# A decoder block on one core: the bias scratch written from all 128 partitions, and the SBUF laid out anew

## The chip, the cores and the metric

The kernel runs on one core of one Trainium2 chip. The metric is device time in microseconds (us), the median of several executions; less is better. "Profile" below is one execution recorded by the hardware profiler, "trace" the list of its instructions, waits and transfers.

## The reference: what is computed

One hybrid decoder block on 256 tokens (SEQ) with a model width of 2048 (D), all in float32:

```python
x = x + 0.5 * swiglu(rms_norm(x, g1), w_gate, w_up, w_down)      # width 2048 -> 5632 -> 2048
h = rms_norm(x, gm)
q, k, v, glu_a, glu_b, gate_a, gate_c = split(h @ w_in)           # 8 heads, two score maps each
o = diff_attention(q1, q2, k1, k2, v, lam, rel_bias_table)        # causal, T5 bias by distance
attn_branch = (rms_norm(o, head_g) * 0.2) @ w_attn_branch
u = causal_depthwise_conv(glu_a * sigmoid(glu_b))                 # 31 taps, 1024 channels
conv_branch = silu(layer_norm(u)) @ w_conv_branch
x = x + (sigmoid(gate_a) * attn_branch + sigmoid(gate_c) * conv_branch) @ w_out
x = x + 0.5 * swiglu(rms_norm(x, g2), ...)                        # a second FFN like the first
return rms_norm(x, final_g)
```

In the attention the score of query position q and key position k gets a bias that depends on the head and on q - k alone: a table of 32 buckets by 8 heads, and -1e30 where k is later than q.

## The kernel before

**Products.** TensorE (PE) does every large product in float32r, a rounded float32. To keep the accuracy, each operand is split into a rounded high part and the rest (hi, lo), and a product is hi*hi + lo*hi + hi*lo. Activations lie transposed as tiles of 128 features by 512 columns: 256 tokens of hi, then 256 of lo, so one such slice is 2 KB in each partition.

- `lin` (L292) multiplies with the weights as the stationary operand. For each k-tile and each of four column tiles it issues a pair: `high` (L305), 512 columns of the activation against `wh`, and `low` (L310), the 256 hi columns against `wl`. It serves both FFNs' up products, the first FFN's down product, the GLU, q, k, and the output projection.
- `lin_tok` (L341) and `tok_products` (L333) turn it round: the activation slice (128 by 128) is stationary and 512 columns of weights move, three matmuls a k-tile (L337 hi*wl, L338 hi*wh, L339 lo*wh). It serves v, the gates, the two branches and the second FFN's down product.

**Weights.** The class `Weights` loads every weight of the model once, in units of 1 MB (four k-tiles by 512 columns), with DMAs on SyncE's queue (SP, L58), three raw buffers `w`. ScalarE (ACT, L87) makes `wh` from a half unit, VectorE (DVE, L88) makes `wl` by subtraction; there are four buffers of each. A new load is issued when a raw buffer has been split. So the splits run a few half units ahead of PE, and the loads two to three units ahead of the splits.

**The order around the bias.** `Side` (L110) runs generators beside the products: each `tick` of `lin` or `lin_tok` advances them at a rate of their own. `bias_rows` (L463) is such a job, one step in ten ticks. It builds in `bias_row` (8 partitions, one for each head, 384 values) the bias by distance, with 32 small copies on GpSimd (POOL, L473), and then issues 8 DMAs on POOL's queue (L477): each takes the 1536 bytes of one head's row, from one partition of SBUF, and writes them 128 times into the DRAM scratch `row_d` (8 x 128 rows of 385 values). Later `bias_load` (L652) reads a head's scratch with rows one value askew, which gives the 128 x 256 tile of biases for a block of queries. POOL also multiplies the gate activations by the norm (L369), in order with these DMAs.

**SBUF.** Pools take their place in the order in which they are made (L142 to L146): `const`, `big`, `wpool`, `work`, `small`. By the allocation of this program, 16 KB of DMA scratch and 128 B of constants come first, then `const` with 2944 B, so `big` begins at byte 19456 of each partition, which is 4 x 4096 + 3072. All tiles of `big` that PE reads are whole multiples of 4 KB long: the residual stream `xT`, the regions P (two tiles of 16 KB: `h1`, `hm`, `mg`, `a2`) and Q (two of 16 KB: `a1`, `qk`, `vo`, `oT`, `cT`, `h2`, `qh`, `ql`), and they all begin at 3072 past a multiple of 4096. `u_sb` (9152 B) lies among them, and so the tiles behind it, `wpool`'s `w`, `wh` and `wl` among them, begin at 4032 past a multiple of 4096: a multiple of 64 B and of nothing larger.

At the very end (L880) the last four half units of weights are not split into `wh` and `wl` but into `qh` and `ql`, which lie in region Q.

`rsqrt` (L248) refines a square root in two scratch tiles of `work`, `rs_v` and `rs_t`; `tmp()` (L236) hands out the five buffers of the tile `t` in turn.

Of the kernel before, what the change touches and what calls it, by code (L numbers as in the profile page):

```python
# [9 lines left out]
F32 = mybir.dt.float32  # L10
# [5 lines left out]
P = 128  # L16
T = 256
D = 2048
FF = 5632
H = 8  # L20
# [5 lines left out]
KU = 4  # L26
KH = 2
NEG = -1e30
LAM_INIT = 0.8 - 0.6 * math.exp(-0.3 * 0)


def bucket(n):
    if n < 16:
        return n
    return min(31, 16 + int(math.log(n / 16) / math.log(8) * 16))
# [98 lines left out]
def block_kernel(  # L134
# [5 lines left out]
    nc = tc.nc  # L140

    const = ctx.enter_context(tc.tile_pool(name="const", bufs=1))  # L142
    big = ctx.enter_context(tc.tile_pool(name="big", bufs=1))
    wpool = ctx.enter_context(tc.tile_pool(name="wpool", bufs=2))
    work = ctx.enter_context(tc.tile_pool(name="work", bufs=2))
    small = ctx.enter_context(tc.tile_pool(name="small", bufs=3))  # L146
    dram = ctx.enter_context(tc.tile_pool(name="dram", bufs=1, space=bass.MemoryType.DRAM))
    psum = ctx.enter_context(tc.tile_pool(name="psum", bufs=5, space=bass.MemoryType.PSUM))
    pmisc = ctx.enter_context(tc.tile_pool(name="pmisc", bufs=3, space=bass.MemoryType.PSUM))
    ctx.enter_context(tc.manual_schedule())  # L150


    groups = [[0, 1, 2, 3], [4, 5, 6, 7], [8, 9, 10]]
# [82 lines left out]
    def tmp():  # L236
        return work.tile([P, T], F32, name="t", tag="t", bufs=5)
# [10 lines left out]
    def rsqrt(dst, src, scale, eps):  # L248

        shape = list(dst.shape)  # L250
        v = work.tile(shape, F32, name="rs_v", tag=f"rsv{shape[-1]}", bufs=1)
        t = work.tile(shape, F32, name="rs_t", tag=f"rst{shape[-1]}", bufs=1)
        nc.vector.tensor_scalar(v, src, scale, eps, ALU.mult, ALU.add)
        nc.scalar.activation(dst, v, AF.Sqrt)
        yield
        nc.vector.reciprocal(dst, dst)
        yield
        nc.vector.tensor_tensor(t, dst, dst, ALU.mult)
        nc.vector.tensor_tensor(t, t, v, ALU.mult)
        yield  # L260
        nc.vector.tensor_scalar(t, t, -0.5, 1.5, ALU.mult, ALU.add)
        nc.vector.tensor_tensor(dst, dst, t, ALU.mult)
        yield
# [11 lines left out]
    def rstd_steps(acc, rstd, n, eps):  # L275
        yield from rsqrt(rstd, mean_d(acc), D / n, eps)
# [181 lines left out]

    row_d = dram.tile([H, P, 385], F32, name="row_d")

    def bias_rows():  # L463
        row = work.tile([H, 384], F32, name="bias_row", tag="s2", bufs=1)

        nc.gpsimd.memset(row[:, 256:384], NEG)
        rel = 0
        while rel < 256:
            end = rel
            while end < 256 and bucket(end) == bucket(rel):  # L470
                end += 1
            b = bucket(rel)
            nc.gpsimd.tensor_copy(row[:, 256 - end:256 - rel], loads["tab"][:, b:b + 1].broadcast_to([H, end - rel]))  # L473
            rel = end
            yield
        for h in range(H):
            nc.gpsimd.dma_start(out=row_d[h:h + 1, :, 0:384], in_=row[h:h + 1].unsqueeze(1).broadcast_to([1, P, 384]))  # L477
            yield


    side.add(bias_rows(), 0.1, delay=256)


# [30 lines left out]

    neglam = small.tile([P, 1], F32, name="neglam", bufs=1)
    U0 = KW - 1
    u_sb = big.tile([P, 8, U0 + T], F32, name="u_sb")
    y_sb = big.tile([P, 8, T], F32, name="y_sb", tag="y")

    def mixer_setup():  # L520
# [6 lines left out]
        nc.vector.tensor_tensor(neglam, e12[:, 0:1], e12[:, 1:2], ALU.subtract)  # L527
        nc.vector.tensor_scalar(neglam, neglam, LAM_INIT, -1.0, ALU.add, ALU.mult)
        nc.vector.tensor_scalar(loads["gh"], loads["gh"], 1.0 - LAM_INIT, None, ALU.mult)
        yield  # L530
# [206 lines left out]
    def attn_finish():  # L737
        nonlocal oT
        rs = small.tile([P, 2 * H], F32, name="rs_o", bufs=1)
        for _ in rsqrt(rs, ss, 1.0 / P, 1e-5):  # L740
            yield
            yield
# [240 lines left out]
```

## Time and profile before

| | us |
|---|---|
| median of 3 runs | 2148.82 (2148.69 to 2148.85) |
| the profiled execution | 2143.47 |
| its span, first to last instruction | 2141.7 |
| PE busy | 2104.0 |
| DVE busy | 1389.4 |
| ACT busy | 1027.7 |
| POOL busy | 189.0 |

The engines run beside each other, so the shares don't add up to the span. "PE" is the matmuls, "PEld" the loads of the stationary operand, which overlap them. Matmuls overlap each other in the trace too: the time that one shows is longer than the distance from its start to the next one's start, and the distance is what a stream of them costs.

### The profile page before, as it was taken

The numbers are of one execution on the slowest core, as the hardware profiler recorded it, in microseconds if no ns is written. First come the engines' busy times: TensorE is split into PE (matmuls) and PEld (weight loads), VectorE is DVE, ScalarE is ACT, GpSimd is POOL, SyncE is SP. The second block draws the span as 40 slices with busy tenths as digits, with TensorE's granted clock in tenths as the row PEclk, the third lists the DMA queues.
The fourth block names the chain that finished last, engine by engine and source line by source line (L and its number), as shares of the span: only waits on it lengthen the run. The fifth ranks groups of instructions, "written<-read, shape, count | busy, mean of one in ns | idle before, by whom it ended". The sixth has DMA issues, their size and how long they took to land. (4 is left out here: it accounts for less than half of the span.)

```text
span 2141.7 us, 28362 instructions
## 1 busy us (share of the span) xinstructions
PE 2104.0 (98%) x11230; PEld 1790.3 (84%) x11230; DVE 1389.4 (65%) x1915; ACT 1027.7 (48%) x1456; POOL 189.0 (9%) x226
## 2 busy tenths in 40 slices
PE   8999999979999999999999999999999999999998
PEld 6888888867888888888778788888888888888887
DVE  8666556635556776789888766665654656545665
ACT  5544344433345555455555744554543444434444
POOL 6101011110011110000000000200100001000011
PEclk9999999989999999999999999999999999999999
DMA  6655555786555555555554555555555555555553
GB/s 236 203 196 180 194 186 189 192 115 214 183 192 179 186 190 197 181 180 178 182 168 169 190 183 177 177 201 192 178 197 180 180 194 193 180 193 177 197 183 132
DMA packets 57446, 395.95 MB, mean 185 GB/s; under 512 B 6864, under 2 KB 6896, under 8 KB 10464
## 3 DMA queue, kind: packets, MB, share of 16 engines
q1 hardware_dynamic: 55872, 390.10, 52.3%
q0 software_dynamic: 1440, 4.03, 2.6%
q8 instruction: 88, 1.44, 0.3%
q14 instruction: 46, 0.38, 0.0%
HBM read 390.43 MB, written 3.67 MB: 184 GB/s over the span
## 5 line engine op out<-in xcount | busy, mean ns | idle before, releaser
L88 DVE TENSOR_TENSOR wl<-w,wh 128x1024 fp32r<-128x1024 f32 x731 | 902.7, 1248 | 607.8 <-ACT wh L87 600.6
L87 ACT ACTIVATE wh<-w 128x1024 fp32r<-128x1024 f32 x731 | 764.8, 1057 | 821.2 <-PE ps_mm L305 546.5
L305 PE MATMUL ps_mm<-h,wh 128*128 128x512 f32 x2816 | 981.7, 396 | 5.9 <-DVE h L229 5.7
L310 PE MATMUL ps_mm<-h,wl 128*128 128x256 f32 x2816 | 762.4, 281 | 3.5 <-DVE wl L88 3.3
L305 PEld LDWEIGHTS ps_mm<-h,wh 128*128 128x128 f32 x2816 | 518.7, 188 | 115.0 <-ACT wh L71 5.7
L310 PEld LDWEIGHTS ps_mm<-h,wl 128*128 128x128 f32 x2816 | 528.1, 188 | 22.3 <-DVE wl L88 5.7
L305 PE MATMUL ps_mm<-a,wh 128*128 128x512 f32 x704 | 246.0, 397 | 18.1 <-ACT wh L87 18.1
L369 POOL TENSOR_TENSOR s_t<-s_t,rstd 128x256 f32<-128x256 f32 x88 | 85.7, 974 | 1201.2 <-ACT s_t L368 1201.2
L310 PE MATMUL ps_mm<-a,wl 128*128 128x256 f32 x704 | 190.9, 282 | 0.5 <-DVE wl L88 0.5
L305 PE MATMUL ps_mm<-hm,wh 128*128 128x512 f32 x512 | 178.9, 396 | 0.0
L305 PEld LDWEIGHTS ps_mm<-a,wh 128*128 128x128 f32 x704 | 130.2, 189 | 45.5 <-ACT wh L87 18.4
L310 PE MATMUL ps_mm<-hm,wl 128*128 128x256 f32 x512 | 138.4, 281 | 0.0
L310 PEld LDWEIGHTS ps_mm<-a,wl 128*128 128x128 f32 x704 | 133.0, 189 | 5.5 <-DVE wl L88 1.0
L337 PE MATMUL ps_mm<-wl,a 128*128 128x512 f32 (+1 forms) x344 | 133.9, 389 | 0.0
L338 PE MATMUL ps_mm<-wh,a 128*128 128x512 f32 (+1 forms) x344 | 133.8, 389 | 0.0
L339 PE MATMUL ps_mm<-wh,a 128*128 128x512 f32 (+1 forms) x344 | 133.8, 389 | 0.0
L337 PE MATMUL ps_mm<-wl,hm 128*128 128x512 f32 x320 | 130.6, 408 | 0.0
L339 PE MATMUL ps_mm<-wh,hm 128*128 128x512 f32 x320 | 126.5, 395 | 0.0
L338 PE MATMUL ps_mm<-wh,hm 128*128 128x512 f32 x320 | 126.4, 395 | 0.0
L305 PEld LDWEIGHTS ps_mm<-hm,wh 128*128 128x128 f32 x512 | 94.4, 188 | 20.4 <-issue 0.7
L571 DVE SCALAR_TENSOR_TENSOR y_sb<-u_sb,cw_sb,y_sb 128x256 f32<-128x256 f32 x240 | 105.3, 478 | 0.0
L354 ACT ACTIVATE rh<-ps_mm 128x256 f32<-128x256 f32 x208 | 77.5, 373 | 45.8 <-PE ps_mm L305 45.7
(192 smaller groups left out, 1808.9 us busy)
## 6 DMA issues: line engine op xcount, KB each, us to landing
w<-in_ffn_w_up_dram SPq DMA_DIRECT2D x88, 1024.0 KB, 4.9
w<-in_ffn_w_down_dram SPq DMA_DIRECT2D x88, 1024.0 KB, 4.8
w<-in_ffn_w_gate_dram SPq DMA_DIRECT2D x85, 1024.0 KB, 4.9
w<-in_w_in_dram SPq DMA_DIRECT2D x72, 1024.0 KB, 4.8
w<-in_w_out_dram SPq DMA_DIRECT2D x16, 1024.0 KB, 4.9
w<-in_w_attn_branch_dram SPq DMA_DIRECT2D x8, 1024.0 KB, 4.8
w<-in_w_conv_branch_dram SPq DMA_DIRECT2D x8, 1024.0 KB, 4.8
w<-in_ffn_w_gate_dram SPq DMA_DIRECT2D x5, 512.0 KB, 8.9
```

Of the source, the lines that this page charges most:

```text
L87: self.nc.scalar.activation(wh, w, AF.Copy)
L88: self.nc.vector.tensor_tensor(wl, w, wh.bitcast(F32), ALU.subtract)
L305: nc.tensor.matmul(ps[ct], lhsT=w, rhs=xs(kt), start=(kt == 0), stop=(kt == nk - 1))
L310: nc.tensor.matmul(ps[ct][:, T:2 * T], lhsT=w, rhs=xs(kt)[:, 0:T], start=False, stop=False)
L337: nc.tensor.matmul(ps, lhsT=hi, rhs=wl[:, kk, :], start=(first and kk == 0), stop=False)
L338: nc.tensor.matmul(ps, lhsT=hi, rhs=wh[:, kk, :], start=False, stop=False)
L339: nc.tensor.matmul(ps, lhsT=lo, rhs=wh[:, kk, :], start=False, stop=(last and kk == KH - 1))
L354: nc.scalar.activation(r, ps[:, T:2 * T], AF.Copy, scale=scale)
L369: nc.gpsimd.tensor_tensor(s, s, rstd, ALU.mult)
L571: nc.vector.scalar_tensor_tensor(y, src, w, y, ALU.mult, ALU.add)
```

## The change

The scratch gets its rows in three steps instead of one. The 8 rows (12 KB) go to a DRAM tile `row_1`; four DMAs read two heads' rows each from there into all 128 partitions of a new SBUF tile `spread` (393 KB each); four DMAs write `spread` to `row_d`, each partition its own copy. `spread` takes the place of region `sga`, which nothing uses until the GLU.

The pools are made in another order: `small` (832 B) moves ahead of `big`, a tile `pad` of 192 B is put behind it, and `u_sb` gets a pool of its own behind `wpool`. With 128 + 2944 + 832 + 192 = 4096, `big` begins at 20480, a multiple of 4096, and so does every tile of `big` and `wpool`. In `rsqrt` the scratch `rs_t` becomes one of the `tmp()` buffers, which makes room.

```diff
--- before.py
+++ after.py
@@ -26,6 +26,7 @@
 KU = 4
 KH = 2
 NEG = -1e30
+PAD = 48
 LAM_INIT = 0.8 - 0.6 * math.exp(-0.3 * 0)
 
 
@@ -140,14 +141,19 @@
     nc = tc.nc
 
     const = ctx.enter_context(tc.tile_pool(name="const", bufs=1))
+    small = ctx.enter_context(tc.tile_pool(name="small", bufs=3))
+
+    pad = ctx.enter_context(tc.tile_pool(name="pad", bufs=1))
     big = ctx.enter_context(tc.tile_pool(name="big", bufs=1))
     wpool = ctx.enter_context(tc.tile_pool(name="wpool", bufs=2))
+    upool = ctx.enter_context(tc.tile_pool(name="upool", bufs=1))
     work = ctx.enter_context(tc.tile_pool(name="work", bufs=2))
-    small = ctx.enter_context(tc.tile_pool(name="small", bufs=3))
     dram = ctx.enter_context(tc.tile_pool(name="dram", bufs=1, space=bass.MemoryType.DRAM))
     psum = ctx.enter_context(tc.tile_pool(name="psum", bufs=5, space=bass.MemoryType.PSUM))
     pmisc = ctx.enter_context(tc.tile_pool(name="pmisc", bufs=3, space=bass.MemoryType.PSUM))
     ctx.enter_context(tc.manual_schedule())
+
+    nc.gpsimd.memset(pad.tile([P, PAD], F32, name="pad"), 0.0)
 
 
     groups = [[0, 1, 2, 3], [4, 5, 6, 7], [8, 9, 10]]
@@ -249,7 +255,7 @@
 
         shape = list(dst.shape)
         v = work.tile(shape, F32, name="rs_v", tag=f"rsv{shape[-1]}", bufs=1)
-        t = work.tile(shape, F32, name="rs_t", tag=f"rst{shape[-1]}", bufs=1)
+        t = tmp()[:, 0:shape[-1]]
         nc.vector.tensor_scalar(v, src, scale, eps, ALU.mult, ALU.add)
         nc.scalar.activation(dst, v, AF.Sqrt)
         yield
@@ -458,6 +464,7 @@
 
 
 
+    row_1 = dram.tile([H, 384], F32, name="row_1")
     row_d = dram.tile([H, P, 385], F32, name="row_d")
 
     def bias_rows():
@@ -473,8 +480,15 @@
             nc.gpsimd.tensor_copy(row[:, 256 - end:256 - rel], loads["tab"][:, b:b + 1].broadcast_to([H, end - rel]))
             rel = end
             yield
-        for h in range(H):
-            nc.gpsimd.dma_start(out=row_d[h:h + 1, :, 0:384], in_=row[h:h + 1].unsqueeze(1).broadcast_to([1, P, 384]))
+        nc.gpsimd.dma_start(out=row_1, in_=row)
+        yield
+        spread = big.tile([P, H, 384], F32, name="spread", tag="sga")
+        for h in range(0, H, 2):
+            nc.gpsimd.dma_start(out=spread[:, h:h + 2], in_=bass.AP(tensor=row_1.tensor, offset=row_1.offset + h * 384,
+                                                                  ap=[[0, P], [1, 2 * 384]]))
+            yield
+        for h in range(0, H, 2):
+            nc.gpsimd.dma_start(out=row_d[h:h + 2, :, 0:384].rearrange("h p c -> p h c"), in_=spread[:, h:h + 2])
             yield
 
 
@@ -514,7 +528,7 @@
 
     neglam = small.tile([P, 1], F32, name="neglam", bufs=1)
     U0 = KW - 1
-    u_sb = big.tile([P, 8, U0 + T], F32, name="u_sb")
+    u_sb = upool.tile([P, 8, U0 + T], F32, name="u_sb")
     y_sb = big.tile([P, 8, T], F32, name="y_sb", tag="y")
 
     def mixer_setup():
```

## Rows read from the trace of the kernel before

**Rows 1.** The page, first lines: span; PE's busy time, share and instructions.

```profile
span 2141.7 us, 28362 instructions
PE 2104.0 (98%) x11230; PEld 1790.3 (84%) x11230; DVE 1389.4 (65%) x1915; ACT 1027.7 (48%) x1456; POOL 189.0 (9%) x226
```

**Rows 2.** Waits of PE over the whole span: us in total, times, longest.

```profile
PE ps_mm L305 <- ACT wh L87: 18.1, 1, 18.1
```

**Rows 3.** Waits of all engines, 440 to 500 us.

```profile
ACT wh L87 <- DMA w<-in_ffn_w_down_dram: 21.2, 2, 20.9
```

**Rows 4.** Timeline of PE, 466 to 492 us: start, duration, instruction, idle before it.

```profile
467.35 0.28 PE L310 MATMUL ps_mm<-a,wl 128*128 128x256 f32 x1
485.71 0.79 PE L305 MATMUL ps_mm<-a,wh 128*128 128x512 f32 x1 [18.08 <-ACT wh L87]
...
490.55 0.46 PE L305 MATMUL ps_mm<-a,wh 128*128 128x512 f32 x1
```

**Rows 5.** DMA, 448 to 483 us: queue's share of 16 engines; issues, median us to landing.

```profile
q0 software_dynamic: 331, 0.98, 78.0%
...
w<-in_ffn_w_down_dram SPq DMA_DIRECT2D x2, 1024.0 KB, 32.4
```

**Rows 6.** DMA issues of the whole span: count, KB each, median us to landing.

```profile
w<-in_ffn_w_up_dram SPq DMA_DIRECT2D x88, 1024.0 KB, 4.9
...
out_dram<-x SPq DMA_DIRECT2D x8, 256.0 KB, 2.7
...
row_d<-bias_row POOLq DMA_DIRECT2D x8, 192.0 KB, 17.2
...
fg<-in_final_norm_g_dram POOLq DMA_DIRECT2D x1, 1024.0 KB, 6.8
```

**Rows 7.** Timeline of POOL, 400 to 480 us.

```profile
403.30 1.09 POOL L477 DMA_DIRECT2D row_d<-bias_row  x2 [0.30 <-POOL bias_row L473]
437.59 0.74 POOL L369 TENSOR_TENSOR s_t<-s_t,rstd 128x256 f32<-128x256 f32 x1 [33.20 <-ACT s_t L368]
...
444.95 2.60 POOL L477 DMA_DIRECT2D row_d<-bias_row  x5
```

**Rows 8.** Timeline of PE, 2108.5 to 2119 us, weights moving: first and last of two runs.

```profile
2108.30 0.39 PE L339 MATMUL ps_mm<-wh,a 128*128 128x512 f32 x1
...
2111.10 0.39 PE L339 MATMUL ps_mm<-wh,a 128*128 128x512 f32 x1
...
2113.17 0.39 PE L339 MATMUL ps_mm<-qh,a 128*128 128x512 f32 x1
...
2116.57 0.39 PE L339 MATMUL ps_mm<-qh,a 128*128 128x512 f32 x1
```

**Rows 9.** Timeline of PE, 2119 to 2123 us: first and last of nineteen 256-column matmuls.

```profile
2120.17 0.28 PE L339 MATMUL ps_mm<-wh,a 128*128 128x256 f32 x1
...
2122.21 0.28 PE L339 MATMUL ps_mm<-wh,a 128*128 128x256 f32 x1
```

**Rows 10.** Two stretches of `lin` alone: length, then busy us and count by engine.

```profile
50.00:185.00 135.00, 135.00 (x773) 118.04 (x772) 84.75 (x110) 66.92 (x100) 24.17 (x42) 1.00 0.56 191
575.00:710.00 135.00, 135.00 (x767) 117.53 (x766) 80.61 (x104) 62.87 (x92) 11.61 (x12) 1.00 0.54 187
```

**Rows 11.** Lines 305 and 337 on PE: count, min/median/max ns, first and last start.

```profile
L305 PE MATMUL ps_mm<-h,wh x2816: 387/396/767, 5.7 to 2066.3; 128*128 128x512 f32 x188
...
L337 PE MATMUL ps_mm<-wl,hm x320: 392/394/587, 911.4 to 1202.5; 128*128 128x512 f32 x160
```

**Rows 12.** Two stretches with the convolution on DVE, columns as in rows 10.

```profile
870.00:1050.00 180.00, 180.00 (x925) 148.05 (x923) 157.36 (x288) 90.28 (x152) 2.14 (x4) 1.00 0.53 182
1050.00:1200.00 150.00, 149.44 (x675) 118.53 (x674) 127.99 (x231) 87.44 (x138) 1.07 (x2) 1.00 0.50 174
```

**Rows 13.** Timeline of POOL, 0 to 6 us.

```profile
1.26 0.20 POOL L214 MEMSET ones<- 128x128 f32 x1
4.12 0.61 POOL L244 TENSOR_TENSOR acc<-xT 128x256 f32<-128x256 f32 x1 [2.67 <-DMA xT<-in_x_dram]
```

## The prediction, made before the change was run

> **What bounds the kernel now.** I read the page's first lines, then the waits of PE, then the one stretch in which PE waits, then how fast PE goes where it doesn't. PE is busy 2104.0 of 2141.7 us, and DVE, the next, 1389.4 [rows 1]. So the end is set by PE, and a change can pay in two ways alone: PE waits less, or its matmuls follow each other faster. Of waits there is one of size: 18.1 us, once, for ACT's `wh` [rows 2]. What idle time is left to PE is small.
>
> The wait lies at 467 us. Between the matmul at 467.35 and the next at 485.71 PE does nothing, and ACT, which PE waits for, itself waits 20.9 us for a weight load [rows 3, 4]. That load took 32.4 us to land, where its kind takes 4.9 [rows 5, 6]. What filled the DMA engines is POOL's queue, 78% of all sixteen from 448 to 483 us, with 0.98 MB [rows 5]: 0.98 MB in 35 us is 28 GB/s. These are the bias DMAs. Two were issued at 403, then POOL stood 33 us behind a gate multiplication that waits for ACT, and five went out within 2.6 us from 445 on [rows 7]. Each reads one partition. 192 KB at 28 GB/s is 7 us, so the five hold the DMA engines until about 483, and PE starts again at 485.7.
>
> The Trainium skill says the same of a single partition: on its page "SBUF — State Buffer", section "Door 1: The DMA port swizzle", four partitions on one port move 27.6 GB/s and all 128 move 328. The 28 GB/s of this trace agrees.
>
> **How fast PE goes.** This is where the second half of the change must act, so I looked for a place in the trace of before where only the address differs. There is one, at the end of the kernel. `tok_products` runs there on the same stationary tile `a2`, with 512 columns moving, first from `wh`/`wl`, then from `qh`/`ql`, with nothing else changed in the loop. From `wh`/`wl` twelve steps take 2.80 us, 233.3 ns each. From `qh`/`ql` fifteen steps take 3.40 us, 226.7 ns each [rows 8]. The first lie at 4032 past a multiple of 4096, which is only a multiple of 64; the second at 3072, a multiple of 1024. So a moving read from the badly placed tiles costs 6.7 ns a matmul. With 256 columns a step from `wl`/`wh` is 113.3 ns (eighteen in 2.04 us), half of 226.7 [rows 9]: there the placement costs nothing, presumably because the stationary load, from the well placed `a2`, takes as long.
>
> Now `lin`. Its moving tiles are well placed (regions P and Q), its stationary ones are `wh`/`wl`. 773 matmuls overlap 135 us, and 767 in another stretch [rows 10]. Taking off the two that reach over the edges, a pair takes 350 ns in the one and 353 in the other. Well placed it should be a step of 512 and one of 256, 226.7 + 113.3 = 340.0 ns. The excess is 10 to 13 ns, and two reads at 6.7 ns are 13.3. So both forms fit one price: about 6.7 ns for each read from the `w` tiles, a little of it hidden in the first stretch.
>
> **The change part by part.**
>
> 1. *The stall.* 485.71 - 467.35 - 0.12 = 18.2 us. After it the matmuls run at half speed for a while: from 485.71 to 490.55 there are six pairs, 4.84 us where 2.1 would do [rows 4], so 2.7 us more. Sum 21 us, if the new transfers don't starve the loads. They are 12 KB, then four reads of 393 KB, then four writes of 393 KB, which is twice the bytes. But a broadcast row into 128 partitions (`fg`, 1 MB) lands in 6.8 us beside the loads, and 256 KB out of 128 partitions lands in 2.7 [rows 6]. By these the 3.15 MB take some 1.6 x 6.8 + 6 x 2.7 = 27 us of latency one after the other, but far less of the engines' time, and they are spread from 403 to about 460 as POOL comes free. The loads were starved only after 22 us of nearly full engines (445 to 467), so I take no stall; the bound on the other side is half of it kept, 10 us. New waits: POOL waits for `row_1` before the reads, and for the reads before the writes, a few us each. Behind them stands nothing before 600 us but the gate multiplications of 437 to 445 us, and their result is read a whole `lin` later (64 pairs, 22 us). Nobody reads `row_d` before 781 us.
>
> 2. *`lin`.* 2816 + 704 + 512 + 256 = 4288 pairs (line 305 has four groups, of which one is shown) [rows 11]. 11.5 ns each, the middle of the two stretches, is 49 us; by the two ends 43 to 56. If only the moving read matters, it is nothing.
>
> 3. *`lin_tok`.* 328 + 320 + 64 + 64 = 776 k-steps with 512 columns from `wh`/`wl` (line 337 has five groups, of which one is shown) [rows 11], three matmuls each: 2328 x 6.67 = 15.5 us.
>
> 4. *The rest.* The memset of `pad`: 0.2 us on POOL, as a larger one takes [rows 13], before a wait of 2.67 us for `x`; nothing. `rs_t` from the `tmp` ring: a DVE step may wait for the user four buffers back, which is done long before; 0 to 1 us. No instruction of PE is added or taken away. DVE is the cover that gets thin: where the convolution runs it is busy 157 of 180 and 128 of 150 us, 87 and 85% [rows 12]. With PE 3% faster this is 90%. If that made PE wait, it would take back at most the gain of these 330 us, 10 us; I take none.
>
> Sum: 21 + 49 + 15.5 = 86 us (rounded). Against the profiled execution's own 2143.5 this gives 2057.5; the median of the runs lies 5.3 us above that execution, and I keep the difference: 2148.8 - 86 = 2063.
>
> **The rivals.**
>
> *A. Stall gone, every read at the good price.* 2063; with the bounds above 2054 to 2075.
>
> *B. The good price is only partly reached in `lin`,* because 512 and 256 columns alternate there. For it: the nine steps between the two runs of rows 8, just behind the change of tiles, take 2.07 us, 230 ns each, so a rhythm has to settle. Against: in `lin` the tile and the rhythm are the same for hundreds of pairs, and the excess in the second stretch is just two reads' price. Half of `lin`'s gain: 2148.8 - 21 - 15.5 - 24.5 = 2088.
>
> *C. The address doesn't matter;* the 6.7 ns belong to the part of the memory in which `wpool` lies, or to what else goes on in it (loads and splits write there). The 256-column row speaks for it a little, since there the bad address costs nothing. Against: line 337 has a median of 394 ns in the gates' stage, with loads and splits beside it, and shows the same 0.39 us at the end of the kernel [rows 8, 11], and the two runs of rows 8 are neighbours. Only the stall goes: 2148.8 - 21 = 2128. The Trainium skill would have it so: "TensorE: Matmul & The Clock Gate", section "Back-to-back issue gap", gives a distance that depends on the columns alone, and "SBUF — State Buffer", section "SBUF: two separate sides", gives PE ports of its own that wait for nobody. By the first rule 512 columns would be an estimated 215.8 ns; the trace has 226.7 and 233.3 and so doesn't agree.
>
> *D. Slower: the reads get in each other's way.* With all tiles at multiples of 4096 the stationary and the moving read of one matmul begin in the same place of their 4 KB. If this made the two streams meet, it would be in the main loop of every stage. No row shows such a meeting, so its price is bounded by nothing here; I take one bad read's 6.7 ns more for each pair and each matmul of `lin_tok`: (4288 + 2328) x 6.67 = 44 us, less the stall's 21: 2148.8 + 23 = 2172. It decides from 21 us / 6616 = 3.2 ns on. Against: in the second run of rows 8 the distance between the stationary and the moving address takes several multiples of 1024, among them multiples of 4096, at one speed.
>
> *E. The scratch doesn't do what it says:* if not the read of one partition but the writing of 1024 short rows to DRAM were the 28 GB/s, the same rows are written now and the stall stays. Against: the final output leaves at 256 KB in 2.7 us [rows 6], though in longer rows. With the good price of the reads 2063 + 21 = 2084.
>
> **How the numbers follow.** A 0.54, B 0.15, C 0.17, D 0.06, E 0.08. The likeliest is A: 2063. A, B and E end below 2100 and hold 0.77, so the range has to take in C: 2054 to 2128. Its lower end is A with `lin` at 56 us and two us of rounding. 0.2% is 4.3 us, about what a measurement of this kernel tells from no change. A, B, C and nearly all of E are faster by more, 0.93; slower is D with a rest, 0.05; within it 0.02.
>
> **What would show it.** The stall: no row of PE waiting for `wh` near 467 us, and weight loads landing in 5 to 10 us there. If E is right, the writes of `spread` take as long as the 17.2 us of the old ones. The reads: the medians of L305 (396 ns) and L337 (394) [rows 11] fall by about 7 ns, steps of L337 are 226.7 ns in all stages, and a pair of L305 and L310 takes 340 ns, so 50 to 185 us holds about 795 matmuls instead of 773. If C is right the medians don't move; if B is right L337 moves and L305 only half. What would make the prediction wrong most is that the stationary read has no such price, since for it there is no pair of rows that differs in the address alone.

## The result, and the profile after

The changed kernel takes 2118.66 us (2117.05 to 2119.28), against 2148.84 (2148.69 to 2149.89) for the kernel before on the same chip: a ratio of 0.9857 [0.984, 0.9874], 30 us less where 86 were forecast. The time lies in the stated range, 2054 to 2128, but the gain is about a third of the forecast one. The profiled execution took 2118.52 us.

In the code after, L311 is `high` (before L305), L316 `low` (L310), L343 to L345 are the three matmuls of `lin_tok` (L337 to L339), and L88 and L89 are the splits.

The page's first lines, answering [rows 1]. The span is 25 us shorter and PE still fills it, DVE's busy time is what it was:

```profile
span 2116.7 us, 28368 instructions
PE 2097.1 (99%) x11230; PEld 1790.2 (85%) x11230; DVE 1389.5 (66%) x1915; ACT 1027.7 (49%) x1456; POOL 190.0 (9%) x228
```

All of PE's waits (us in total, times, longest), answering [rows 2]:

```profile
PE ps_mm L311 <- DVE h L235: 6.0, 2, 5.8
PE ps_mm L316 <- DVE wl L89: 3.0, 4, 1.9
PE ps_mg L837 <- DVE sg L832: 0.9, 1, 0.9
PE ps_mean L273 <- DVE acc_c L594: 0.9, 1, 0.9
```

The 18.1 us for `wh` are gone. The DMA view of 448 to 483 us, answering [rows 5]: POOL's queue takes 19.5% of the engines for 2.37 MB where it took 78.0% for 0.98, and weight loads land in 4.9 us instead of 32.4. The writes of `spread` carry 384 KB in 9.2 us; the old writes needed 17.2 for 192 KB [rows 6].

```profile
q0 software_dynamic: 614, 2.37, 19.5%
...
w<-in_ffn_w_down_dram SPq DMA_DIRECT2D x7, 1024.0 KB, 4.9
row_d<-spread POOLq DMA_DIRECT2D x4, 384.0 KB, 9.2
spread<-row POOLq DMA_DIRECT2D x2, 384.0 KB, 6.8
```

Now PE's pace. Three stretches of the kernel after: the two of [rows 10], `lin` alone, and one of `lin_tok` alone. Columns: length, then busy us and count of PE, PEld, DVE, ACT and POOL, granted clock, DMA share, GB/s.

```profile
50.00:185.00 135.00, 135.00 (x766) 117.14 (x766) 85.40 (x111) 66.17 (x99) 25.62 (x43) 1.00 0.57 194
575.00:710.00 135.00, 135.00 (x766) 117.10 (x765) 84.46 (x114) 65.81 (x99) 12.32 (x13) 1.00 0.54 185
...
1845.00:1880.00 35.00, 35.00 (x157) 28.96 (x156) 17.13 (x15) 13.43 (x14) 0.00 (x0) 1.00 0.59 202
```

And the third stretch in the kernel before:

```profile
1845.00:1880.00 35.00, 35.00 (x152) 28.05 (x151) 18.89 (x19) 14.22 (x15) 0.00 (x0) 1.00 0.56 190
```

`lin_tok` went from 152 matmuls in 35 us to 157: less the two at the edges, 233.3 ns each before and 225.8 after. (Such a count is good to one matmul: 1.5 ns for `lin_tok` here, 0.5 ns for a pair of `lin` in 135 us.) `lin` did not get 795 matmuls into 135 us, but 766, a pair in 353.4 ns. That is the slower of the two paces that it had before (773 and 767), now in both stretches.

The durations tell the same, answering [rows 11] (min/median/max ns). `lin_tok`'s median falls from 394 to 389 ns, `lin`'s rises from 396 to 398:

```profile
L311 PE MATMUL ps_mm<-h,wh x2816: 388/398/765, 5.8 to 2042.2; 128*128 128x512 f32 x188
```
```profile
L343 PE MATMUL ps_mm<-wl,hm x320: 387/389/577, 897.6 to 1184.9; 128*128 128x512 f32 x160
```

Two stretches of PE's timeline (start, duration) show where `lin`'s gain was lost. The first is a piece of `lin`, the second the end of the kernel, which answers [rows 8, 9]:

```profile
639.77 0.40 PE L311 MATMUL ps_mm<-h,wh 128*128 128x512 f32 x1
640.01 0.28 PE L316 MATMUL ps_mm<-h,wl 128*128 128x256 f32 x1
640.12 0.40 PE L311 MATMUL ps_mm<-h,wh 128*128 128x512 f32 x1
640.37 0.28 PE L316 MATMUL ps_mm<-h,wl 128*128 128x256 f32 x1
640.49 0.40 PE L311 MATMUL ps_mm<-h,wh 128*128 128x512 f32 x1
640.72 0.28 PE L316 MATMUL ps_mm<-h,wl 128*128 128x256 f32 x1
...
641.89 0.40 PE L311 MATMUL ps_mm<-h,wh 128*128 128x512 f32 x1
```
```profile
2094.81 0.28 PE L343 MATMUL ps_mm<-wl,a 128*128 128x256 f32 x1
...
2096.85 0.28 PE L345 MATMUL ps_mm<-wh,a 128*128 128x256 f32 x1
...
2102.44 0.39 PE L343 MATMUL ps_mm<-wl,a 128*128 128x512 f32 x1
...
2104.93 0.39 PE L345 MATMUL ps_mm<-wh,a 128*128 128x512 f32 x1
```

At the end of the kernel (where `qh`/`ql` hold the first four of the last eight half units, so that `wh`/`wl` come back behind them) 512 columns from `wl`/`wh` are at the good pace: eleven steps in 2.49 us, 226.4 ns. But seventeen steps of 256 columns take 2.04 us, 120.0 ns each, where before it was 113.3 [rows 9]. The placement that makes 512 columns 6.7 ns faster makes 256 columns 6.7 ns slower, and a pair of `lin` is one of each: by these steps 233.3 + 113.3 = 346.7 ns before and 226.7 + 120.0 = 346.7 after. (They are steps with the weights moving; in `lin` the weights are stationary. Experiment 2 has the steps of `lin` itself for the kernel after; for the kernel before no run has them.) In `lin` neither sum is reached: six pairs from 639.77 to 641.89 us take 2.12 us, 353.3 ns, and the steps of the high go 0.24, 0.25, 0.23 us, again and again.

### The profile page after: what moved, and what is told of

It is laid out like the page before. It is cut to its first block, busy times and chain, and to the rows that moved or that the text cites. A ratio compares the mean times of both kernels' runs of the same rounds, so it can differ in the third digit from the quotient of the medians.

```text
span 2116.7 us, 28368 instructions
## 1 busy us (share of the span) xinstructions
PE 2097.1 (99%) x11230; PEld 1790.2 (85%) x11230; DVE 1389.5 (66%) x1915; ACT 1027.7 (49%) x1456; POOL 190.0 (9%) x228
## 5 line engine op out<-in xcount | busy, mean ns | idle before, releaser
L89 DVE TENSOR_TENSOR wl<-w,wh 128x1024 fp32r<-128x1024 f32 x731 | 902.7, 1248 | 581.4 <-ACT wh L88 578.6
L88 ACT ACTIVATE wh<-w 128x1024 fp32r<-128x1024 f32 x731 | 765.3, 1057 | 794.7 <-PE ps_mm L311 553.2
L311 PE MATMUL ps_mm<-h,wh 128*128 128x512 f32 x2816 | 986.7, 400 | 6.0 <-DVE h L235 6.0
L316 PE MATMUL ps_mm<-h,wl 128*128 128x256 f32 x2816 | 762.8, 282 | 3.3 <-DVE wl L89 3.0
L311 PEld LDWEIGHTS ps_mm<-h,wh 128*128 128x128 f32 x2816 | 519.5, 189 | 119.4 <-ACT wh L72 5.7
L316 PEld LDWEIGHTS ps_mm<-h,wl 128*128 128x128 f32 x2816 | 532.7, 189 | 22.8 <-DVE wl L89 5.2
L311 PE MATMUL ps_mm<-a,wh 128*128 128x512 f32 x704 | 245.4, 398 | 0.0
L316 PE MATMUL ps_mm<-a,wl 128*128 128x256 f32 x704 | 189.9, 281 | 0.0
L311 PE MATMUL ps_mm<-hm,wh 128*128 128x512 f32 x512 | 180.1, 400 | 0.0
L311 PEld LDWEIGHTS ps_mm<-a,wh 128*128 128x128 f32 x704 | 129.2, 188 | 28.2
L316 PE MATMUL ps_mm<-hm,wl 128*128 128x256 f32 x512 | 138.4, 281 | 0.0
L316 PEld LDWEIGHTS ps_mm<-a,wl 128*128 128x128 f32 x704 | 132.9, 189 | 4.7
L343 PE MATMUL ps_mm<-wl,a 128*128 128x512 f32 (+1 forms) x344 | 132.1, 384 | 0.0
L345 PE MATMUL ps_mm<-wh,a 128*128 128x512 f32 (+1 forms) x344 | 132.1, 384 | 0.0
L343 PE MATMUL ps_mm<-wl,hm 128*128 128x512 f32 x320 | 129.5, 405 | 0.0
L345 PE MATMUL ps_mm<-wh,hm 128*128 128x512 f32 x320 | 125.3, 392 | 0.0
L311 PEld LDWEIGHTS ps_mm<-hm,wh 128*128 128x128 f32 x512 | 94.4, 188 | 21.4 <-issue 0.7
```

The source lines that it names most:

```text
L88: self.nc.scalar.activation(wh, w, AF.Copy)
L89: self.nc.vector.tensor_tensor(wl, w, wh.bitcast(F32), ALU.subtract)
L311: nc.tensor.matmul(ps[ct], lhsT=w, rhs=xs(kt), start=(kt == 0), stop=(kt == nk - 1))
L316: nc.tensor.matmul(ps[ct][:, T:2 * T], lhsT=w, rhs=xs(kt)[:, 0:T], start=False, stop=False)
L343: nc.tensor.matmul(ps, lhsT=hi, rhs=wl[:, kk, :], start=(first and kk == 0), stop=False)
L345: nc.tensor.matmul(ps, lhsT=lo, rhs=wh[:, kk, :], start=False, stop=(last and kk == KH - 1))
```

## The experiments

Each time stands beside the kernel before on the same chip: medians of 2146.41, 2145.84, 2149.18 and 2147.8 us in four groups (runs from 2142.62 to 2150.2). The changed kernel stands beside 2148.84 in a group of its own, so a difference of two or three us against it says little. "Pair" is a high and a low of `lin`, read from 50 to 185 us as above; `lin_tok` from 1845 to 1880 us. Where it says "the starts give", it is the mean of the distances from start to start within `lin` or `lin_tok`, without those that hold a wait or another matmul (over 280 ns for 512 columns, over 140 for 256).

**1. One part at a time.** Against the changed kernel, first the new scratch in the old layout, then the new layout with the old scratch:

```diff
-    small = ctx.enter_context(tc.tile_pool(name="small", bufs=3))
-    pad = ctx.enter_context(tc.tile_pool(name="pad", bufs=1))
...
-    upool = ctx.enter_context(tc.tile_pool(name="upool", bufs=1))
+    small = ctx.enter_context(tc.tile_pool(name="small", bufs=3))
...
-        t = tmp()[:, 0:shape[-1]]
+        t = work.tile(shape, F32, name="rs_t", tag=f"rst{shape[-1]}", bufs=1)
...
-    u_sb = upool.tile([P, 8, U0 + T], F32, name="u_sb")
+    u_sb = big.tile([P, 8, U0 + T], F32, name="u_sb")
```

```diff
-        nc.gpsimd.dma_start(out=row_1, in_=row)
...
-        for h in range(0, H, 2):
-            nc.gpsimd.dma_start(out=row_d[h:h + 2, :, 0:384].rearrange("h p c -> p h c"), in_=spread[:, h:h + 2])
+        for h in range(H):
+            nc.gpsimd.dma_start(out=row_d[h:h + 1, :, 0:384], in_=row[h:h + 1].unsqueeze(1).broadcast_to([1, P, 384]))
```

> The scratch in three steps, on the layout of before. Theory of two separate parts: only the stall at 467 us goes, so 21 us by the trace of before and up to 26 if the runs without the profiler stalled longer: 2122 to 2128 us, no row of PE waiting for wh near 467 us, steps of lin_tok still 233.3 ns, pairs of lin between 349 and 354 ns. If the new transfers starve the loads in part, a shorter wait stays and the time is 2130 to 2140.

> The new layout with the old scratch, each row written from one partition. Theory: the stall of 18 us comes back and lin_tok keeps its steps of 226.7 ns, with pairs of lin at 353.3 as in the changed kernel: 2118.7 + 21 to 26 = 2140 to 2145 us. If the layout took away part of the stall by itself, 2119 to 2130.

The scratch alone: 2125.05 us (2121.67 to 2127.53), ratio 0.99 [0.9878, 0.9922], 21 us less. The layout alone: 2139.46 (2137.68 to 2140.49), 0.9967 [0.9956, 0.9978], 7 us less, and the stall is back. From PE's waits:

```profile
PE ps_mm L311 <- ACT wh L88: 18.4, 1, 18.4
```

The two parts add up to the whole (21 + 7 of 30) as far as the intervals tell, so neither takes much from the other, and the missing gain is the layout's. With the new layout in both, the scratch is worth 2139.46 - 2118.66 = 20.8 us.

**2. The order of `lin`, not its addresses.** If the pace is a rhythm of 512 and 256 columns, another order must move it at the same addresses. First, runs of two (per column tile high, high, low, low):

```diff
-                for i in range(len(pair) * KH):
-                    if pair[0] * KH + i < nk - 1:
-                        high(ct, i)
-                        low(ct, i)
-                    else:
-                        low(ct, i)
-                        high(ct, i)
+                for i in range(0, len(pair) * KH, KH):
+                    two = range(i, i + KH)
+                    for f in (high, low) if pair[0] * KH + i + KH < nk else (low, high):
+                        for j in two:
+                            f(ct, j)
```

> The changed kernel, with the order of matmuls in lin changed: for each column tile two of 512 columns, then two of 256, instead of one and one. Theory R (the cost is in the change between the widths, whatever the address): half as many changes, so a pair falls from 353.3 to about 347 ns, 4288 x 6 = 26 us, 2093 us. Theory S (each stationary read from wh and wl costs its 6.7 ns whatever the order): 353 ns and 2119 us.

2102.41 us (2101.46 to 2102.74), 0.9799 [0.9784, 0.9814]: 16 us faster than the changed kernel. The stretch of 50 to 185 us holds 776 matmuls, a pair in 348.8 ns:

```profile
50.00:185.00 135.00, 135.00 (x776) 117.87 (x775) 86.14 (x112) 67.25 (x100) 25.61 (x43) 1.00 0.58 197
```

Then runs of eight, all highs of a half unit over the four column tiles and then all lows:

```diff
+            for i in range(0, len(pair) * KH, KH):
+                end = pair[0] * KH + i + KH == nk
+                for f in (low, high) if end else (high, low):
+                    for ct in range(4):
+                        for j in range(i, i + KH):
+                            f(ct, j)
```

> The changed kernel, with eight matmuls of 512 columns over the four column tiles and then eight of 256. Theory R: within a lin a pair comes to 340 (226.7 + 113.3) to 346.7 ns (226.7 + 120.0, the steps at the end of the changed kernel), 28 to 57 us, 2062 to 2091; the four results of a lin are now ready within 2 us, so at its end PE may wait for banks of PSUM, which could take back up to 1 us for each of 68 lins. Theory S: 353 ns inside a lin, 2119 us or more.

2196.11 us (2195.38 to 2196.61), 1.0236 [1.022, 1.0252]: slower, and for another reason. Its largest waits of PE:

```profile
PE ps_mm L311 <- DVE t L361: 29.4, 42, 1.3
PE ps_mm L311 <- DVE s_t L361: 25.9, 41, 0.9
```

At the end of a `lin` all four result tiles in PSUM, the memory that PE writes to, now become ready together, and the next `lin` waits until they are read out (L361). Between these waits the starts of the matmuls give 349.1 ns a pair, no better than runs of two. So longer runs bring the pair no further, and the order at the end of a `lin` matters by itself.

This run also has what the trace of before lacked, long streams of one width in `lin`, with the weights stationary. In the new layout the sixth to eighth high of a run start 227 ns apart and the lows behind the first 119 to 121 ns (some 400 of each): the 226.7 and 120.0 of the kernel's end hold for `lin` too. The first five highs behind a run of lows take 228 to 236 ns; that is where the change of widths is paid.

**3. Which tiles' placement.** The `wl` tiles alone moved 64 B on, in the order of the changed kernel and in runs of two:

```diff
+    padl = ctx.enter_context(tc.tile_pool(name="padl", bufs=1))
+    lpool = ctx.enter_context(tc.tile_pool(name="lpool", bufs=2))
+    nc.gpsimd.memset(padl.tile([P, 16], F32, name="padl"), 0.0)
-        wl = self.pool.tile([P, KH, CK], F32R, name="wl", tag="wl", bufs=self.bufs)
+        wl = self.lpool.tile([P, KH, CK], F32R, name="wl", tag="wl", bufs=self.bufs)
```

> The changed kernel with the four wl tiles moved by 64 B (wh and all else stay). Theory M (the stationary and the moving read of neighbouring matmuls meet, and what counts is the difference of their addresses: streams of 512 columns want 0, as the 226.7 against 233.3 ns of lin_tok, streams of 256 want 64, as the 113.3 of the old layout's end against the 120.0 of the new one's): in lin the steps of 256 columns, whose stationary tile is wl, get cheaper, a pair falls from 353.3 to 340 to 347 ns, 28 to 57 us, and lin_tok's third matmul with wl moving goes back to 233.3, 776 x 6.7 = 5 us: 2067 to 2096. Theory R alone (only the alternation of widths costs, the address of the stationary tile nothing): lin stays at 353 and the time is 2124.

> As the one before, and two matmuls of 512 columns, then two of 256, as in the run with runs of two (2102 us, 349.0 ns a pair). Theory M: 340 to 345 ns, 2102 - 17 to 39 + 5 = 2068 to 2090. Theory R alone: 349, 2107.

2125.51 us (2124.01 to 2126.76), 0.9902 [0.9885, 0.992], and 2115.91 (2115.49 to 2117.49), 0.9859 [0.9845, 0.9874]: 7 and 13.5 us slower than with `wl` in its place. Theory M is refuted, since nothing got faster. R alone comes near in the first run (2124), but not in the second (2107). A stretch of `lin` and one of `lin_tok` of the first:

```profile
50.00:185.00 135.00, 135.00 (x767) 116.94 (x766) 85.37 (x111) 66.42 (x99) 25.59 (x43) 1.00 0.58 195
...
1845.00:1880.00 35.00, 35.00 (x153) 28.32 (x152) 18.11 (x17) 12.84 (x13) 0.00 (x0) 1.00 0.57 198
```

The pair stays at 352.9 ns (in runs of two the starts give 350.0), and `lin_tok` goes back to 35/151 = 231.8 ns. There the starts give 231 to 232 ns for each of its three lines, though `wl` is read by one of them alone: 2328 x 4.5 = 10 us, where the expectations had 5. So here the pace belongs to the stream of the three lines and not to the one matmul whose operand was moved.

**4. All of PE's tiles 64 B on.** Does the multiple of 4 KB count, or only how the tiles lie to each other?

```diff
-PAD = 48
+PAD = 64
```

> The changed kernel with all of big and wpool moved by 64 B together, so that every tile begins 64 past a multiple of 4096 and the differences stay. Theory M (differences): steps of 226.7 in lin_tok and pairs of 353.3, 2118 us. Rival (the moving read itself wants a multiple of 128 or more): steps of 233.3 in lin_tok as in the kernel before, 2118 + 13 to 15 = 2133.

One run, 2119.33 us, within the changed kernel's runs but for 0.05 us. Both paces are the changed kernel's:

```profile
50.00:185.00 135.00, 135.00 (x766) 117.09 (x765) 85.53 (x111) 65.93 (x98) 25.61 (x43) 1.00 0.57 193
...
1845.00:1880.00 35.00, 35.00 (x156) 28.96 (x156) 17.14 (x15) 13.79 (x13) 0.00 (x0) 1.00 0.57 195
```

None of PE's large tiles begins at a multiple of 4 KB here, nor of 128 B. So the multiple does nothing; what is left is the difference between the addresses.

**5. Runs of two in the old layout** (the first kernel of 1 with the order of 2):

> The old layout with the new scratch (2125 us, pairs between 349 and 354 ns) and lin in runs of two. If the gain of runs of two does not need the new layout, a pair falls to about 349 ns on the mean, some 4 ns x 4288 = 16 us, 2108 us, and the runs scatter less. If it needs it, 2120 to 2127.

2098.95 us (2097.47 to 2099.24), 0.9778 [0.9763, 0.9792]: 20 us faster than the changed kernel, with its layout left out.

```profile
50.00:185.00 135.00, 135.00 (x784) 118.78 (x783) 86.96 (x112) 67.55 (x102) 25.65 (x43) 1.00 0.58 197
...
1845.00:1880.00 35.00, 35.00 (x152) 28.20 (x151) 16.98 (x16) 13.78 (x13) 0.00 (x0) 1.00 0.55 194
```

A pair in 135/391 = 345.3 ns, faster than the new layout in any order tried, and faster than either case of the expectation; `lin_tok` at 233.3. For `lin` the old placement is the better one.

**6. The difference, several in one kernel.** Gaps between the activation regions, with `lin` in runs of two, so that one execution has several differences against the same weights. First four of them:

```diff
+    gaps = {"P1": 384, "Q0": 64, "Q1": 32, "end": 32}
+    def gap(tag):
+        n = gaps.pop(tag, 0)
+        if n:
+            nc.gpsimd.memset(big.tile([P, n // 4], F32, name=f"gap_{tag}"), 0.0)
     def region(r, i, shape, dtype, name):
+        gap(f"{r}{i}")
```

> The changed kernel with `lin` in runs of two (as in the run in which both highs go ahead of both lows), and with small gaps between the four activation regions, so that region P's first tile (h, a2 of k-tiles 0 to 7) begins 512 B below wh and wl (modulo 4 KB), P's second tile 128 B below, Q's first tile (a1, oT) 64 B below and Q's second (a1, cT) 32 B below. All four cases stand in one run, against the same wh and wl. If the pace hangs on the difference modulo 128 B, as the runs so far allow: 512 and 128 go like difference 0 (349.0 ns a pair in lin, 226.7 ns a matmul in lin_tok), 64 like the old layout (345.2 and 233.3), and 32 like one of them or between. If a larger unit counts (the old layout differed by 960, and only multiples of 4096 have been tried as 'difference 0' in lin), 512 and 128 go otherwise too. If not the difference but the place of the weights or of the activation counts, all four go at one pace. By the middle one the time is about 2102 to 2104 us: only a1 (704 pairs) and 384 of the lin_tok matmuls change pace.

One run, 2108.76 us, where 2102 to 2104 was expected (the expectation counts `a1` alone on Q; `h2` lies there too, with 1408 pairs more). In `lin_tok` on `a2` at the kernel's end, the first tile (512 B below) has 156 matmuls in 35 us, 227.3 ns; the second (128 B below) takes ten steps in 2.32 us, 232 ns (L349 to L351 are the three matmuls of `lin_tok` here):

```profile
2035.00:2070.00 35.00, 35.00 (x156) 29.01 (x155) 23.65 (x25) 19.04 (x20) 0.00 (x0) 1.00 0.57 192
```
```profile
2092.78 0.39 PE L350 MATMUL ps_mm<-wh,a 128*128 128x512 f32 x1
...
2095.10 0.39 PE L351 MATMUL ps_mm<-wh,a 128*128 128x512 f32 x1
```

So 512 goes as 0 does, and 128 does not: modulo 128 falls. By the starts of all of `lin_tok` it is 227.7 ns at 512 B below, 232.5 at 128, 228.9 at 64 and 233.3 at 32. For `lin` the starts give 348.3 ns a pair at 512 B below, 350.4 at 128, 347.3 at 64 and 350.8 at 32; at difference 0, in the runs of two of experiment 2, they give 348.5 on the first tile of a region and 349.5 on the second. The old layout's difference is -960, which modulo 512 is 64 ahead, not 64 below; if that is the whole of it, -448, which is 64 ahead modulo 512 too, must bring both of its paces back:

```diff
+    gaps = {"Q0": 64, "end": 448}
```

> The changed kernel with `lin` in runs of two and 64 B between regions P and Q; 448 B behind Q bring wh and wl back to P's phase. Region Q (a1, oT, cT, h2) then begins 64 B ahead of wh and wl modulo 512 (the old layout's difference, -960, is the same modulo 512 and 1024), region P (h1, hm, mg, a2) 0 ahead. If the difference modulo some 512 B sets the pace, both paces stand in one run: lin on P (2176 pairs) at 349.0 ns a pair, lin on Q (2112 pairs) at the 345.2 of the old layout in runs of two; lin_tok on P 226.7 ns, on Q (oT and cT, 384 matmuls) 233.3. Against the 2102.4 us of runs of two in the new layout this is 2112 x 3.8 ns = 8.0 us less and 384 x 6.67 ns = 2.6 us more: 2097, about the 2099 of the old layout in runs of two. If the sign or the whole distance counts and not the difference modulo 512, Q goes at another pace, as the 347.2 ns at 64 B below.

2097.0 us (2095.82 to 2097.62), 0.9765 [0.975, 0.9779], the 2097 expected. Stretches of `lin` on P, `lin` on Q, `lin_tok` on P and (1175 to 1210 us) `lin_tok` on Q:

```profile
50.00:185.00 135.00, 135.00 (x776) 117.80 (x775) 84.98 (x111) 67.53 (x100) 24.14 (x42) 1.00 0.57 191
...
1662.00:1797.00 135.00, 135.00 (x785) 118.73 (x784) 84.79 (x111) 66.28 (x98) 11.64 (x12) 1.00 0.55 188
1845.00:1880.00 35.00, 35.00 (x157) 28.96 (x156) 16.77 (x16) 13.79 (x13) 0.00 (x0) 1.00 0.56 184
```
```profile
1175.00:1210.00 35.00, 35.00 (x152) 28.20 (x151) 22.68 (x22) 22.08 (x24) 0.00 (x0) 1.00 0.59 194
```

On P 348.8 and 225.8 ns, on Q 344.8 and 233.3: the paces of the new and of the old layout side by side in one execution, from one gap of 64 B. (On Q the changed kernel has 227 ns by the starts, so it is not the stage that makes `lin_tok` slow there.) It is the fastest kernel of the study, though its interval and that of experiment 5 overlap.

**7. `wl` alone by 448 B,** so that the low's activation is 64 ahead of it modulo 512 and the high's at difference 0:

```diff
-    nc.gpsimd.memset(padl.tile([P, 16], F32, name="padl"), 0.0)
+    nc.gpsimd.memset(padl.tile([P, 112], F32, name="padl"), 0.0)
```

> The changed kernel with `lin` in runs of two and the wl tiles alone 448 B further on (the earlier run had them 64 B further on: 349.8 ns a pair, 232.0 ns in lin_tok). The low product's activation is then 64 B ahead of wl modulo 512, as in the old layout, the high product's at difference 0. If each matmul had a pace of its own by its own two addresses, the lows would be those of the old layout and the highs those of the new one, and a pair would be 226.7 to 233 + 113.3 to 116, below 349. If the pace belongs to the sequence as a whole, as the run with wl by 64 showed for lin_tok (all three lines slowed, though the addresses of two were unchanged), the pair stays near 349 and lin_tok near 232, and the time near the 2115.9 of that run.

2100.65 us (2099.27 to 2101.32), 0.9783 [0.9767, 0.98]. 779 matmuls in 135 us, a pair in 347.5 ns, and `lin_tok` 35/153 = 228.8 ns:

```profile
50.00:185.00 135.00, 135.00 (x779) 118.31 (x778) 85.17 (x111) 67.88 (x100) 24.30 (x43) 1.00 0.58 193
...
1845.00:1880.00 35.00, 35.00 (x155) 28.71 (x153) 17.64 (x17) 13.77 (x13) 0.00 (x0) 1.00 0.57 197
```

Neither expectation fits whole. Paces between the two layouts' are possible, and the pair does not get near the 340 ns that the best step of each width would give.

## Why the prediction was wrong

*Step 1, the stall: right.* 21 us forecast, 21 measured (the scratch alone, 2146.41 to 2125.05; in the new layout 20.8). The loads land in time during the new transfers. E is refuted by POOL's queue, 2.37 MB in 19.5% of the engines' time where 0.98 MB took 78.0%: the same rows, written from 128 partitions, don't hold the engines.

*Step 3, `lin_tok`: right in size, not in its reason.* 233.3 to 226.7 was forecast for 2328 matmuls, 15.5 us. The starts of all matmuls of the three lines give a mean of 233.3 before and 227.5 after, 2328 x 5.8 = 13.5 us; the rest would be the slower steps behind a change of tiles or widths. But the prediction laid the 6.7 ns on tiles that begin at a multiple of 64 B only. In experiment 4 they do, and the pace is the good one. What set the two runs of [rows 8] apart is the difference: `qh`/`ql` and `a2` both lie at 3072, at a difference of 0, `wh`/`wl` at one of -960. The change brought the difference to 0 together with the multiple of 4 KB, so the sum came out.

*Step 4: right.* DVE, which was to get thin, makes PE wait for 0.9 us at one place of the convolution (`acc_c`), 0.6 before.

*Step 2, `lin`: wrong, in size and in sign.* 49 us less was forecast. By the starts of its matmuls a pair takes 352.9 ns after, against a mean of 351.3 before: 4288 x 1.6 = 7 us more. The step that failed is "both forms fit one price: about 6.7 ns for each read from the `w` tiles". It was worked out by taking 340.0 ns as the well placed pair, and a part of that sum, the 113.3 ns of 256 columns, came from a row of the badly placed tiles [rows 9]. The prediction read the row as "there the placement costs nothing". There was no row of 256 columns at the new placement; when there was one, it said 120.0. Of the 13.3 ns between 340.0 and the 353.3 of the timeline above, this is 6.7. The other 6.7 is what the alternation costs, a term that the likeliest case put at nothing: runs of two take 4.6 of it away at the same addresses (353.4 to 348.8 ns, experiment 2).

So the missing gain has two halves: the fast 512 and the fast 256 do not meet in the new layout, and the change between the widths has a price of its own. What made up the 350 to 353 ns of the old layout is not shown. That it was 6.7 for the 512 columns and the rest for the alternation would fit the kernel's end [rows 8, 9], but there the weights move, and no run has a long stream of one width in `lin` at the old placement.

*The offset.* "I keep the difference" of 5.3 us between the median and the profiled execution. It was no constant: the runs of before range over 2142.62 to 2150.2 us, and its trace has stretches of `lin` at both paces of [rows 10]. After, all runs lie within 2.2 us and both stretches have one pace. So the 30 us between the medians are 25 between the profiled executions: 21 and 13 less, 7 and some 2 more. That 2118.66 lies in the range at all is luck: its upper end was there for rival C, which did not happen.

*The rivals.* None happened as told. B had the right place (the rhythm of 512 and 256 columns), but took it for something that costs half of a gain; there was no gain in it. C, that the address doesn't matter, is refuted by 225.8 and 233.3 ns in one execution of experiment 6. So the runs do not agree with the formula that C names from the Trainium skill ("TensorE: Matmul & The Clock Gate", "Back-to-back issue gap"), which has no term but the columns: at one granted clock, 1.00, streams of 512 columns were seen at 226.7 and at 233.3 ns and streams of 256 at 113.3 and at 120.0. D expected `lin` and `lin_tok` both to suffer where addresses coincide; `lin_tok` is fastest there, and `lin` lost 1.6 ns a pair where D took 6.7. The chance given to A, 0.54, rested on a fit with one unknown and two numbers, neither of which varied the stationary address alone.

*What is shown, and what stays open.* Shown: the difference between the addresses of activation and weights changes PE's pace, with differences of 0 and -512 alike, and -960 and -448 alike; a multiple of 4 KB as such does nothing (one run); the order of the widths changes the pace at fixed addresses. Open is what in the chip does it: that the loads of the stationary operand and the reads of the moving one meet in the same memory would fit, but no run here separates it from another cause. The period is open too: 256 was not tried, and inside the tiles the slices of one stream lie 512 B apart themselves (the column tiles of `lin`, the two halves of the tokens in `lin_tok`), so a period above 512 would look much the same here. Nor is it shown why 256 columns like another difference than 512.

## What to carry to other kernels

A price read from one pair of rows holds for the form of instruction in these rows: before it is multiplied by thousands of another form, look for a row of that form in both conditions, and where there is none, keep a zero and a negative price in the likeliest case and not in a rival alone. Where PE is the bound and its matmuls are of two widths, the order in which they follow each other was worth more here (16 us from runs of two) than the placement (7 us), at the cost of a few lines. And when a layout is tuned, what to vary is the distance between the tiles that are read together, in small steps, for each form by itself.

## What the runs showed of the hardware

- With the weights moving, one 512-column float32r matmul follows another at 226.7 or 233.3 ns at the same clock and with no wait, by 64 B modulo 512 in the distance of the operands (-512 or -448 B in one execution of experiment 6). One of 256 columns follows at 113.3 ns at a distance of -960, where 512 columns have their bad pace, and at 120.0 at a distance of 0, where they have their good one.
- An alternating stream settles into fixed cycles: in the changed kernel mostly of three pairs, highs of 0.24, 0.25 and 0.23 us. The old layout's alternation had two paces, 350 and 353 ns, and took now the one and now the other: of the two profiled executions in that layout, that of before has 351.3 ns on the mean and that of the scratch alone 352.3, 4 us over all of `lin`. That this is the scatter of its other runs too (7.6 us, against 2.2 after) would fit, but is not shown.
- Moving the tile of one of three lines by 64 B slowed all three by about 5 ns (experiment 3).
- A row written 128 times from one partition held the DMA engines at 28 GB/s [rows 5]; read into 128 partitions and written from there, twice the bytes left the weight loads at 4.9 us instead of 32.4 and PE without a wait for `wh`.
